# Strassen matmul with leaky ReLU on one core: the sixth product of six regions split into seven quarter products, like the seventh

## The chip, the cores and the metric

The kernel runs on one core of one Trainium2 chip. The metric is device time in microseconds (us) of one execution. The kernel before took 1568.02 us as the median of three runs (1567.33 to 1568.79).

Engines, as the profile names them: PE multiplies (its matmuls) and PEld loads the stationary operand of a matmul; DVE does elementwise sums and 32x32 transposes; ACT copies and squares; POOL and SP here only issue DMAs. PE writes its sums into PSUM, eight banks of 128 x 512 numbers in f32.

## The reference

```python
def setup_inputs():
    m, k, n = 4096, 4096, 4096
    return {"a": np.random.randn(m, k).astype(np.float32),
            "b": np.random.randn(k, n).astype(np.float32),
            "alpha": np.float32(0.01)}

def reference(a, b, alpha):
    x = np.matmul(a, b)
    return np.where(x > 0, x, alpha * x)
```

One product of two 4096 x 4096 matrices, and a leaky ReLU on the result.

## The kernel before

**Regions.** The output is cut into 16 regions of 1024 x 1024, four row groups g of four columns j. Region (0, 0) is done plainly, while the first data arrive (L279). The other 15 go through one loop (`for i, (g, j) in enumerate(regions)`, L665), the rows of a group in the order 2, 0, 1, 3 (2, 0, 3, 1 for g = 2). The last region of a group is called turning: in it the next group's rows of A are fetched and transposed. (3, 3) is the final one.

**Seven products.** In a region A is cut into 2 x 2 blocks of 512 x 2048 and B into 2 x 2 blocks of 2048 x 512, all in f16, and the four output blocks of 512 x 512 come from seven block products in place of eight (Strassen's scheme in Winograd's form). In the order of the list `PRODUCTS` their left operands are a11, a12, s2, s3, s1, a22 and s4, where s1 to s4 are sums of blocks of A; the right operands are blocks of B and sums of them, which DVE makes in place (`b_sum`, L561). A whole product is 64 matmuls of 128 x 128 by 512 columns (`product`, L672): the contraction runs over two halves k of eight chunks c each, and for each chunk over four row tiles mt, each with a PSUM bank of its own. This text counts the products from one: the sixth is a22's, the seventh s4's.

**The seventh in quarters.** In nine regions (`in_quarters`, L767: g > 0, neither turning nor final) the seventh product is cut by the same scheme once more (`quarters_product`, L696): seven quarter products of 16 matmuls with 256 columns (`part`, L707, its matmuls at L711). They need four sums of quarters of s4, made by DVE once a group (`sums_s4`, L649), kept in DRAM (`kept_s`) and loaded again by SP in the group's other two regions (L824), and four sums of quarters of B22 (`sums_b`, L640). The seven quarters follow each other in this order: two with s4 alone, then sums 4, 2, 1 and 3 of s4, and last `part(x[1, 1], f(4), onto(1, 0))` (L728). Two banks of z (`acc` is z's third, `other` its fourth) take some of the quarters; ACT copies `acc` into SBUF (L718, L721, L726) and DVE adds `other` to that (L723, L727); the rest goes straight onto y.

**Banks.** The eight PSUM banks are two sets of four, y and z. The first, third, fifth and seventh product go into y, the second into z, the fourth and sixth into z anew. The sets change places from one region to the next (`ybank`, L669): the first product of a region writes the four banks that were z in the region before. A product's results leave a bank by an ACT copy into an SBUF tile (`keep`, L690) or by a DVE add onto such a tile (`add`, L733); `leave` (L737) then does the leaky ReLU on DVE (L307) and the store on SP.

**What sets the order.** The kernel is recorded with a manual schedule: every engine and every DMA queue works through its instructions in the order of the code, and the framework adds the waits: for an operand, for a buffer or a bank still being read, and for a DMA's landing. A tile of a pool takes the buffer of its tag that comes free first. SBUF pools that matter here: x (three large buffers: s1, s4 and, by turns, s2 and the rooms of the quarter sums; s2 is kept in DRAM as `kept_s2` and loaded again at each quartered region's end, L867), a16 (three buffers of 128 x 2048 in f16: quarter sums of A, squares of `Measure`, rows of A on the way in), b (two buffers for each block of B) and c (f32 results).

**The rest.** POOL fetches the next region's blocks of B (`fetch_b`, L488), each half k as soon as its buffer is free. `Measure` (squares on ACT at L227, sums on DVE at L236 to L260) takes row and column norms of the blocks; `judge` decides with them at the end whether the f16 result stands. `MEASURED` and `EARLY` say in which region and place each block is measured.

Of the kernel before, what the change touches and what calls it, by code (L numbers as in the profile page):

```python
# [46 lines left out]
def kernel(  # L47
# [440 lines left out]
    def fetch_b(i, quads):  # L488

        if i >= len(regions):  # L490
            return
        for half, nt in quads:
            for u in (2 * half, 2 * half + 1):
                fetch_unit(i, u, nt)
# [79 lines left out]
    def judge():  # L574
# [29 lines left out]
        (1, 2): (None, [A11], None, None), (1, 0): (B21, [B22, A12], None, None),  # L604
        (1, 1): (B21, [B22, A22], None, None),
        (2, 2): (None, [A11], None, None), (2, 0): (A12, [], None, None),
        (2, 3): (B21, [B22, A22], None, None),
        (3, 2): (None, [A11], None, None), (3, 0): (A12, [A22], None, None),
    }
# [8 lines left out]
    kept_s = dram_pool.tile([4, P, KC * HALF], DT, name="kept_s")  # L618
    kept_s2 = dram_pool.tile([P, 2 * KC * RM], DT, name="kept_s2")
    side = 0  # L620

    def quarter_a(t):
        return t.rearrange("p (c m e) -> p c m e", m=HALF, e=2)

    def rooms(i):

        two = x_pool.tile([P, 2, 2, KC * HALF], DT, name="q", tag="x")
        two = [two[:, 0], two[:, 1]]
        three = [a16_pool.tile([P, KC * HALF], DT, name="sq4", tag="a16") for _ in range(3)]
        tq = {2: two[0][:, 0], 1: two[0][:, 1], 4: two[1][:, 0]}  # L630
        sq = {1: three[0], 2: three[1], 3: three[2], 4: two[1][:, 1]}
        return tq, sq

    def quarters_b(i):
        return {(k, n): have_b[i, 2 + k, 1][:, :, n * HALF:(n + 1) * HALF] for k in range(2) for n in range(2)}

    def quarters_s4(g):
        return {(h, k): s[g, "s4", k][:, :, h * HALF:(h + 1) * HALF, :] for h in range(2) for k in range(2)}

    def sums_b(i, tq):  # L640
        y = quarters_b(i)
        f = lambda n: tq[n].rearrange("p (c n) -> p c n", n=HALF)
        tt = nc.vector.tensor_tensor
        tt(y[0, 1], y[1, 1], y[0, 1], SUB)
        tt(f(2), y[0, 1], y[0, 0], ADD)
        tt(f(1), y[1, 1], f(2), SUB)
        tt(f(4), y[1, 0], f(2), SUB)

    def sums_s4(g, sq):  # L649
        x = {key: q.rearrange("p c m e -> p c (m e)") for key, q in quarters_s4(g).items()}  # L650
        f = lambda n: sq[n].rearrange("p (c m) -> p c m", m=2 * HALF)
        tt = nc.vector.tensor_tensor
        tt(f(1), x[1, 0], x[1, 1], ADD)
        tt(f(2), f(1), x[0, 0], SUB)
        tt(f(3), x[0, 0], x[1, 0], SUB)
        tt(f(4), x[0, 1], f(2), SUB)
        for n in range(4):
            nc.sync.dma_start(kept_s[n], sq[n + 1])
# [5 lines left out]

    for i, (g, j) in enumerate(regions):  # L665
        final = i == len(regions) - 1
# [5 lines left out]
        def product(n, banks, first):  # L672
            name, half, nt = PRODUCTS[n]
            todo = [(k, c) for k in range(2) for c in range(KC)]
# [3 lines left out]
            for mt, k, c in order:  # L678
                t = operand(g, name, k)
                nc.tensor.matmul(  # L680
                    banks[mt], a_cols(t, c, mt, t is first_a), B(half, nt, k)[:, c, :],
                    start=first and (k, c) == (0, 0), stop=(k, c) == (1, KC - 1), skip_group_check=not first,
                )
# [6 lines left out]
        def keep(banks, side):  # L690
            _, kept = new_c(side)
            for mt in range(MT):
                nc.scalar.copy(kept[mt], banks[mt])  # L693
            return kept

        def quarters_product(i, y, acc, other, tq, sq):  # L696

            pairs, kept = new_c(side)
            block = lambda r, n: pairs[r][:, :, n * HALF:(n + 1) * HALF]
            b = quarters_b(i)  # L700
            x = quarters_s4(g)
            f = lambda n: tq[n].rearrange("p (c n) -> p c n", n=HALF)
            into = lambda bank: [bank[:, m * HALF:(m + 1) * HALF] for m in range(2)]
            onto = lambda r, n: [y[2 * r + m][:, n * HALF:(n + 1) * HALF] for m in range(2)]
            pair = lambda bank: bank.rearrange("p (m n) -> p m n", m=2)

            def part(xq, yq, to, first=False):  # L707
                for c in range(KC):
                    for m in range(2):
                        rows = slice(m * P, (m + 1) * P)  # L710
                        nc.tensor.matmul(  # L711
                            to[m], xq[:, c // 2, rows, c % 2], yq[:, c, :],
                            start=first and (c, m) == (0, 0), stop=c == KC - 1, skip_group_check=True,
                        )

            part(x[0, 1], b[1, 0], onto(0, 0))
            part(x[0, 0], b[0, 0], into(acc), True)
            nc.scalar.copy(block(0, 0), pair(acc))  # L718
            part(quarter_a(sq[4]), b[1, 1], onto(0, 1))
            part(quarter_a(sq[2]), f(2), into(acc))  # L720
            nc.scalar.copy(block(0, 1), pair(acc))  # L721
            part(quarter_a(sq[1]), f(1), into(other), True)
            nc.vector.tensor_add(block(0, 1), pair(other), block(0, 1))  # L723
            part(quarter_a(sq[3]), b[0, 1], into(acc))
            for n in (1, 0):
                nc.scalar.copy(block(1, n), pair(acc))  # L726
            nc.vector.tensor_add(block(1, 1), pair(other), block(1, 1))  # L727
            part(x[1, 1], f(4), onto(1, 0))  # L728
# [4 lines left out]
        def add(acc, banks):  # L733
            for mt in range(MT):
                nc.vector.tensor_add(acc[mt], banks[mt], acc[mt])  # L735
# [31 lines left out]
        in_quarters = g > 0 and not turning and not final  # L767
        early = measure(i, *EARLY[g, j]) if (g, j) in EARLY else None
        if early:
            early.begin()  # L770
        if first_of_group and g:
            nc.sync.dma_start(kept_s2, whole_s[g, "s2"].rearrange("p k c m e -> p (k c m e)"))
# [6 lines left out]
        u1 = keep(y, side)  # L779
        for k in range(2):  # L780
            b_sum(B(0, 1, k), B(1, 1, k), B(0, 1, k), SUB)
            b_sum(B(0, 0, k), B(0, 1, k), B(0, 0, k), ADD)
        if middle:
            middle.end()
        fetch_a(0, 0)
# [3 lines left out]
        if first_of_group:  # L789
            sum_a(g, "s3")  # L790
        leave(u1, 0, 0)
        for k in range(2):
# [7 lines left out]
        u2 = keep(y, 1 - side)  # L800
        for k in range(2):
# [5 lines left out]
        if late_ones:  # L807
            late_ones[0].end()

        z = [new_bank(zbank + mt) for mt in range(MT)]  # L810
        product(3, z, True)
        v = keep(z, side)
        fetch_b(i + 1, [(0, 1)])
# [4 lines left out]
        if in_quarters:  # L818
            tq, sq = rooms(i)
            if first_of_group:  # L820
                sums_s4(g, sq)
            else:
                for n in (4, 2, 1, 3):
                    nc.sync.dma_start(sq[n], kept_s[n - 1])  # L824
            if len(late_ones) < 2:
                sums_b(i, tq)
# [8 lines left out]
        add(v, y)  # L835
        leave(v, 1, 1)
        if in_quarters and len(late_ones) == 2:
            sums_b(i, tq)
# [6 lines left out]
        fetch_b(i + 1, [(0, 0)])  # L845
# [3 lines left out]
        product(5, z, False)  # L849
# [103 lines left out]
```

## Time and profile before

| | |
|---|---|
| median of three runs | 1568.02 us |
| the profiled execution | 1567.84 us |
| its span, first to last instruction | 1565.9 us |
| granted clock of PE | 0.999 |
| PE, DVE, ACT, POOL busy | 1554.8, 1055.6, 372.4, 299.7 us |
| region (1, 0) from its first to the next region's first matmul | 508.03 to 603.14 us |

The profile comes from one execution, 0.18 us under the median. Its page gives each engine's busy time; the groups give, by line and shape, the number of instructions, the mean time of one and the engine's idle time ahead of them; the timeline lists instructions in order of time, neighbours of one kind merged, with start and length in us and, in brackets, idle time and what ended it. Matmuls overlap each other in the pipeline, so the 379 ns that the groups give for one is longer than the distance from one to the next; the distance is read from the timeline, as starts of consecutive groups over the number of matmuls between.

### The profile page before, as it was taken

How to read it: one execution, taken by the hardware profiler on the slowest of the kernel's cores; microseconds unless marked ns; L12 is line 12 of the kernel's file. 1: busy time of each engine (PE TensorE's matmuls, PEld its weight loads, DVE VectorE, ACT ScalarE, POOL GpSimd, SP SyncE). 2: the span in 40 equal slices, each digit the busy share in tenths (PEclk: the TensorE clock that was granted, in tenths of full speed). 3: DMA queues.
4: the chain of work that ended last, by engine and by line, in shares of the span. 5: the costliest groups of instructions: out<-in, count | busy, mean ns of one | idle time of the engine just before them, and what ended most of it. 6: DMA issues, size and time to landing. Idle time of an engine off the chain costs nothing. (4 is left out here: it accounts for less than half of the span.)

```text
span 1565.9 us, 19332 instructions
## 1 busy us (share of the span) xinstructions
PE 1554.8 (99%) x7707; PEld 753.0 (48%) x7707; DVE 1055.6 (67%) x1172; ACT 372.4 (24%) x390; POOL 299.7 (19%) x482
## 2 busy tenths in 40 slices
PE   9999999999999999999999999999999999999998
PEld 4444444444445445454444545545444454544543
DVE  4378758767975776766789682774868959372533
ACT  2201243612120334401221220531022143110110
POOL 5641110244002011023401102012330110201100
PEclk9999999999999999999999999999999999999999
DMA  9999795999829589499975949769995793949902
GB/s 244 186 217 185 151 279 150 190 194 203 284 54 246 157 167 237 92 249 209 183 275 114 276 135 174 176 140 276 168 235 203 170 260 96 217 144 193 210 27 84
DMA packets 199142, 291.84 MB, mean 186 GB/s; under 512 B 17281, under 2 KB 154753, under 8 KB 193666
## 3 DMA queue, kind: packets, MB, share of 16 engines
q0 software_dynamic: 149376, 141.59, 57.4%
q1 hardware_dynamic: 49378, 148.53, 25.4%
q8 instruction: 62, 1.02, 0.3%
q10 hardware_dynamic: 288, 0.39, 0.1%
q14 instruction: 38, 0.31, 0.1%
HBM read 341.84 MB, written 88.08 MB: 275 GB/s over the span
## 5 line engine op out<-in xcount | busy, mean ns | idle before, releaser
L680 PE MATMUL ps<-b,a 128*128 128x512 f16 x3840 | 836.1, 379 | 0.0
L680 PEld LDWEIGHTS <-a 128*128 128x128 f16 x3840 | 375.7, 98 | 451.1
L680 PE MATMUL ps<-b,s 128*128 128x512 f16 x2304 | 503.2, 379 | 0.0
L680 PEld LDWEIGHTS <-s 128*128 128x128 f16 x2304 | 225.4, 98 | 271.9
L561 DVE TENSOR_TENSOR b<-b 128x4096 f16<-128x4096 f16 x112 | 252.8, 2290 | 94.9 <-DMA b<-in_b_dram 80.0
L505 POOL DMA_DIRECT2D b<-in_b_dram x184 | 136.3, 746 | 940.9 <-PE ps L680 635.7
L735 DVE TENSOR_TENSOR c<-ps,c 128x512 f32<-128x512 f32 x180 | 111.6, 683 | 168.4 <-PE ps L680 110.1
L693 ACT COPY c<-ps 128x512 f32<-128x512 f32 x180 | 92.3, 598 | 538.5 <-PE ps L680 431.0
L139 DVE STREAM_TRANSPOSE a<-a 128x512 uint32<-128x512 uint32 (+2 forms) x120 | 126.3, 1101 | 90.5 <-DMA a<-in_a_dram 89.8
L130 POOL DMA_DIRECT2D a<-in_a_dram x252 | 137.5, 553 | 196.5 <-DVE a L139 122.5
L307 DVE SCALAR_TENSOR_TENSOR c<-c 128x512 f32<-128x512 f32 x240 | 149.5, 686 | 12.7 <-ACT c L880 10.0
L227 ACT ACTIVATE sq<-b 128x2048 bf16<-128x2048 f16 x64 | 119.1, 1910 | 89.8 <-DVE sq L236 75.8
L279 PE MATMUL ps<-b,a 128*128 128x512 f16 x512 | 112.8, 379 | 2.1 <-DMA b<-in_b_dram 0.9
L227 ACT ACTIVATE sq<-a 128x2048 bf16<-128x2048 f16 x48 | 88.8, 1921 | 77.2 <-DVE sq L236 60.3
L279 PEld LDWEIGHTS <-a 128*128 128x128 f16 x512 | 49.7, 98 | 63.0 <-issue 2.9
L718 ACT COPY c<-ps 128x512 f32<-128x512 f32 x9 | 5.3, 586 | 244.2 <-PE ps L711 244.2
L236 DVE TENSOR_TENSOR sq<-sq 128x2048 bf16<-128x2048 bf16 x27 | 33.0, 1223 | 28.8 <-ACT sq L227 28.8
L711 PEld LDWEIGHTS <-s 128*128 128x128 f16 x432 | 42.2, 98 | 6.8
L239 DVE TENSOR_TENSOR sq<-sq 128x2048 bf16<-128x2048 bf16 x27 | 33.1, 1225 | 17.2 <-ACT sq L227 17.2
L711 PEld LDWEIGHTS <-sq 128*128 128x128 f16 x432 | 42.3, 98 | 4.8
L238 DVE TENSOR_TENSOR sq<-sq 128x2048 bf16<-128x2048 bf16 x27 | 33.1, 1226 | 4.7 <-ACT sq L227 2.3
L880 ACT COPY c<-ps 128x512 f32<-128x512 f32 x24 | 12.6, 598 | 98.0 <-PE ps L680 98.0
(86 smaller groups left out, 559.7 us busy)
## 6 DMA issues: line engine op xcount, KB each, us to landing
b<-in_b_dram POOLq DMA_DIRECT2D x192, 512.0 KB, 10.5
out_dram<-c SPq DMA_DIRECT2D x240, 256.0 KB, 6.5
a<-in_a_dram POOLq DMA_DIRECT2D x244, 128.0 KB, 5.5
b<-kept SPq DMA_DIRECT2D x24, 1024.0 KB, 8.5
s<-kept_s SPq DMA_DIRECT2D x9, 2048.0 KB, 10.4
sq<-kept_s SPq DMA_DIRECT2D x18, 512.0 KB, 7.1
b<-in_b_dram POOLq DMA_DIRECT2D x24, 256.0 KB, 9.2
kept<-b SPq DMA_DIRECT2D x6, 1024.0 KB, 7.7
```

The source lines that it names most:

```text
L130: nc.gpsimd.dma_start(a16[32 * q:32 * q + 32], src.rearrange("(g i) w -> i g w", i=32))
L139: nc.vector.transpose(part.rearrange("p c m e -> p c (m e)").bitcast(U32) .rearrange("p c (g i) -> p g c i", i=32), src[:, :, i * n:(i + 1 ...
L227: nc.scalar.activation(to, self.parts[n], SQUARE)
L238: nc.vector.tensor_add(total, total, more[1])
L279: nc.tensor.matmul(ps, a_cols(at[0, h, u], c, mt, (h, u) == (0, 0)), bt[0, u, nt][:, c, :], start=first, stop=last,)
L307: nc.vector.scalar_tensor_tensor(t, t, alpha, t, op0=MULT, op1=MAX if alpha <= 1 else MIN)
L505: nc.gpsimd.dma_start(t[:, c:c + 4, :], b_rows(j, u, c, 4, nt, g > 0))
L561: nc.vector.tensor_tensor(f(to), f(x0), f(x1), op)
L680: nc.tensor.matmul(banks[mt], a_cols(t, c, mt, t is first_a), B(half, nt, k)[:, c, :], start=first and (k, c) == (0, 0), stop=(k, c) == (1 ...
L693: nc.scalar.copy(kept[mt], banks[mt])
L711: nc.tensor.matmul(to[m], xq[:, c // 2, rows, c % 2], yq[:, c, :], start=first and (c, m) == (0, 0), stop=c == KC - 1, skip_group_check=True,)
L735: nc.vector.tensor_add(acc[mt], banks[mt], acc[mt])
```

## The change

**The sixth product in quarters.** In the six quartered regions that are not the first of their group (`both`: (1, 0), (1, 1), (2, 0), (2, 3), (3, 0), (3, 1)) the sixth product becomes seven quarter products too (`sixth_in_quarters`). Sums of quarters of a22 are made once a group, in its first region, kept in DRAM (`kept_q`) and loaded in the other two. The four z banks are taken anew for it, so the fourth product, kept as v, is added to u2 in SBUF ahead of it, and the results of the seven quarters are added from PSUM onto u2 by eight adds of 128 x 512 (`more`). The sums for the seventh product follow into the same seven rooms quarter by quarter: each sum of s4 is loaded, and each sum of B22 made, when the quarter that used the room is done.

**The seventh.** Its order is now: two with s4 alone, sum 4, `x[1, 1]` with t(4), sums 2, 1 and last sum 3. Its accumulating banks are z's fourth (`one`, where `acc` was z's third) and z's second (`other`).

**k turned round.** Behind a quartered region the halves k go in the order (1, 0): fetches of B, sums of B, matmuls. s2 is loaded in two halves, the second behind the first sum of B in the next region (a small DVE memset of the room stands ahead of it).

**Moved.** s3 is made ahead of the second product. The measurements of a few blocks move to other regions.

```diff
     MEASURED = {
         (0, 1): (None, [A11], B12, B11), (0, 2): (B21, [B22, A22], B12, A12),
-        (1, 2): (None, [A11], None, None), (1, 0): (B21, [B22, A12], None, None),
-        (1, 1): (B21, [B22, A22], None, None),
-        (2, 2): (None, [A11], None, None), (2, 0): (A12, [], None, None),
-        (2, 3): (B21, [B22, A22], None, None),
+        (1, 0): (A12, [B22], None, None), (1, 1): (A22, [A11], None, None),
+        (2, 0): (B21, [A12], None, None), (2, 3): (A22, [A11], None, None),
         (3, 2): (None, [A11], None, None), (3, 0): (A12, [A22], None, None),
+        (3, 1): (B21, [B22], None, None), (3, 3): (B21, [B22], None, None),
     }
...
+    def sums_of_a(g, name, room):
...
+        def make(n, x0, x1, op):
+            made[n] = room(n)
...
+            nc.vector.tensor_tensor(f(n), f(x0), f(x1), op)
+            nc.sync.dma_start(kept_q[name][n - 1], made[n])
+
+        make(1, (1, 0), (1, 1), ADD)
+        make(2, 1, (0, 0), SUB)
+        make(3, (0, 0), (1, 0), SUB)
+        make(4, (0, 1), 2, SUB)
...
+    def load_s2(g, k, later=False):
+
+        t = s[g, "s2", k]
+        if later:
+            nc.vector.memset(t[:, 0, :1, :1], 0.0)
+        nc.sync.dma_start(t.rearrange("p c m e -> p (c m e)"), kept_s2[k])
...
+        ks = (1, 0) if in_quarters else (0, 1)
+        late_s2 = in_quarters
...
+        def sixth_in_quarters(pairs, banks, v, y, tq, sq):
...
+            one, other, third, fourth = banks
...
+            quarter_product(x[0, 0], b[0, 0], into(one), True)
+            add(v[:2], y[:2])
+            more(0, 0, one)
+            add(v[2:], y[2:])
+            quarter_product(sx(1), t(1), into(other), True)
+            more(1, 1, other)
+            following(4)
+            next_t[2] = tq[1]
+            quarter_product(x[0, 1], b[1, 0], into(fourth), True)
+            leave(v, 1, 1)
+            quarter_product(sx(2), t(2), into(one))
+            following(2)
+            more(0, 1, one)
+            sums_of_b(y7, next_t, (2,))
+            more(0, 0, fourth)
+            quarter_product(sx(4), b[1, 1], into(other))
+            following(1, sq[4])
+            next_t[4] = tq[2]
+            sums_of_b(y7, next_t, (4,))
+            more(0, 1, other)
+            quarter_product(x[1, 1], t(4), into(third), True)
+            next_t[1] = tq[4]
+            sums_of_b(y7, next_t, (1,))
+            more(1, 0, third)
+            quarter_product(sx(3), b[0, 1], into(one))
+            following(3)
+            more(1, 0, one)
+            more(1, 1, one)
+            return next_t, next_s
...
-            part(x[0, 1], b[1, 0], onto(0, 0))
-            part(x[0, 0], b[0, 0], into(acc), True)
-            nc.scalar.copy(block(0, 0), pair(acc))
-            part(quarter_a(sq[4]), b[1, 1], onto(0, 1))
-            part(quarter_a(sq[2]), f(2), into(acc))
-            nc.scalar.copy(block(0, 1), pair(acc))
-            part(quarter_a(sq[1]), f(1), into(other), True)
+            quarter_product(x[0, 1], b[1, 0], onto(0, 0))
+            quarter_product(x[0, 0], b[0, 0], into(one), True)
+            nc.scalar.copy(block(0, 0), pair(one))
+            quarter_product(sx(4), b[1, 1], onto(0, 1))
+            quarter_product(x[1, 1], t(4), onto(1, 0))
+            quarter_product(sx(2), t(2), into(one))
+            nc.scalar.copy(block(0, 1), pair(one))
+            quarter_product(sx(1), t(1), into(other), True)
             nc.vector.tensor_add(block(0, 1), pair(other), block(0, 1))
-            part(quarter_a(sq[3]), b[0, 1], into(acc))
+            quarter_product(sx(3), b[0, 1], into(one))
             for n in (1, 0):
-                nc.scalar.copy(block(1, n), pair(acc))
+                nc.scalar.copy(block(1, n), pair(one))
             nc.vector.tensor_add(block(1, 1), pair(other), block(1, 1))
-            part(x[1, 1], f(4), onto(1, 0))
             for mt in range(MT):
                 nc.vector.tensor_add(kept[mt], y[mt], kept[mt])
...
+        both = in_quarters and not first_of_group
...
+        if first_of_group:
+            sum_a(g, "s3")
         fetch_a(0, 0)
 
         product(1, z, True)
         add(u1, z)
-        if first_of_group:
-            sum_a(g, "s3")
...
+        if first_of_group and g:
+            sums_of_a(g, "a22", new_a16)
+        if in_quarters:
+            t = x_pool.tile([P, 4, QUARTER], DT, name="q", tag="x")
+            tq, sq = {2: t[:, 0], 1: t[:, 1], 4: t[:, 2]}, {4: t[:, 3]}
+        if both:
+            for n in (1, 2, 3):
+                sq[n] = new_a16()
+            load_sums("a22", sq, (1, 2, 3, 4))
...
+        if both:
+            t3_of_b(quarters_of_b(i, 1, 0))
+            sums_of_b(quarters_of_b(i, 1, 0), tq)
+            t3_of_b(quarters_of_b(i, 1, 1))
+            for mt in range(MT):
+                nc.vector.tensor_add(u2[mt], u2[mt], v[mt])
+        elif in_quarters:
+            sums_of_a(g, "s4", lambda n: sq.setdefault(n, sq[4] if n == 4 else new_a16()))
+            t3_of_b(quarters_of_b(i, 1, 1))
+            sums_of_b(quarters_of_b(i, 1, 1), tq)
...
-        product(5, z, False)
-        fetch_b(i + 1, [(1, 0)])
-        add(u2, z)
+        if not both:
+            product(5, z, False)
+            add(u2, z)
+        fetch_b(i + 1, [(1, 0)], (1, 0) if both else ks)
...
-            kept_c = quarters_product(i, y, new_bank(zbank + 2), new_bank(zbank + 3), tq, sq)
-            fetch_b(i + 1, [(1, 1)])
-            t = new_s(g, "s2")
-            nc.sync.dma_start(t.rearrange("p k c m e -> p (k c m e)"), kept_s2)
+            kept_c = seventh_in_quarters(y, new_bank(zbank + 3), new_bank(zbank + 1), tq, sq)
+            fetch_b(i + 1, [(1, 1)], (1, 0))
+            new_s(g, "s2")
+            load_s2(g, 1)
             leave(kept_c, 0, 1)
```

`quarter_product` is the old `part`; `following` takes a free a16 room (or the one named) and loads the next sum of s4 into it; `load_sums` loads sums from `kept_q`; `t3_of_b` is the in-place sum of `sums_b`, `sums_of_b` its other three; `late_s2` makes the next region's `load_s2(g, ks[1], True)` follow its first `b_sum`.

## The prediction

> **What bounds the kernel now.** First the page's busy times and the group of the whole products:
>
> ```profile
> PE 1554.8 (99%) x7707; PEld 753.0 (48%) x7707; DVE 1055.6 (67%) x1172; ACT 372.4 (24%) x390; POOL 299.7 (19%) x482
> PEclk9999999999999999999999999999999999999999
> L680 PE MATMUL ps<-b,a 128*128 128x512 f16 x3840 | 836.1, 379 | 0.0
> ```
>
> PE has no idle time ahead of these matmuls: the kernel is its stream of matmuls, and the rest costs only where it holds that stream. So I read the timeline of one quartered region, (1, 0), next: its sixth and seventh product and the next region's first.
>
> ```profile
> 577.10 13.98 PE L680 MATMUL ps<-b,a 128*128 128x512 f16 x64
> ...
> 590.91 3.66 PE L711 MATMUL ps<-b,s 128*128 128x256 f16 x32
> ...
> 599.65 1.91 PE L711 MATMUL ps<-b,sq 128*128 128x256 f16 x16
> ...
> 601.39 1.91 PE L711 MATMUL ps<-q,s 128*128 128x256 f16 x16
> 601.59 1.07 ACT L726 COPY c<-ps 128x512 f32<-128x512 f32 x2 [2.91 <-PE ps L711]
> ...
> 602.21 0.69 DVE L727 TENSOR_TENSOR c<-ps,c 128x512 f32<-128x512 f32 x1 [1.62 <-ACT c L726]
> ...
> 603.14 7.07 PE L680 MATMUL ps<-b,a 128*128 128x512 f16 x32
> ```
>
> A whole product takes 590.91 - 577.10 = 13.81 us (215.8 ns a matmul), one in quarters 603.14 - 590.91 = 12.23 (109.2 ns), a quarter 1.747. The reader should also see what happens at the end: sum 3's quarter ends at 601.39, two ACT copies and a DVE add read its banks until 602.90, and only the last quarter (601.39 to 603.14), which goes onto y, stands between that and the next region's first product, which writes these banks. The cover is 0.24 us longer than the work.
>
> The third view is the timeline of (3, 2), the first region of group 3, where DVE is fullest, then the DMA view of that stretch:
>
> ```profile
> 1236.20 1.22 DVE L653 TENSOR_TENSOR sq<-s 128x2048 f16<-128x2048 f16 x1
> 1237.45 2.71 SPq L658 DMA_DIRECT2D kept_s<-sq  x3
> ...
> 1245.66 2.48 DVE L735 TENSOR_TENSOR c<-ps,c 128x512 f32<-128x512 f32 x4
> ...
> 1259.38 2.48 DVE L735 TENSOR_TENSOR c<-ps,c 128x512 f32<-128x512 f32 x4 [8.84 <-PE ps L680]
> ...
> 1259.83 3.66 PE L711 MATMUL ps<-b,s 128*128 128x256 f16 x32
> ```
>
> ```profile
> kept_s<-sq SPq DMA_DIRECT2D x3, 512.0 KB, 5.4
> ...
> kept_s<-q SPq DMA_DIRECT2D x1, 512.0 KB, 10.9
> ```
>
> **The change part by part.**
>
> 1. *The sixth product.* Six times 13.81 becomes 12.23: 6 x 1.58 = 9.5 us less on PE. The seventh's number of matmuls stays.
>
> The Trainium skill ("TensorE: Matmul & The Clock Gate", section "Back-to-back issue gap") speaks against this: it gives about 131 ns a matmul for 512 columns and 81 for 128 as the sustained rate. Estimated from that page, 64 matmuls would take 8.4 us and 112 of 256 columns (some 98 ns) 10.9, a loss of 15 us over six regions. This trace's 215.8 and 109.2 ns decide otherwise.
>
> 2. *The hand-over at a region's end.* The seventh's order is turned: sum 3's quarter is now last. What ran under the old last quarter has no cover: when sum 3's quarter ends, ACT copies `one` (0.20 us later, 1.07 for two), DVE adds `other` behind the first copy, and ends 602.90 - 601.39 = 1.51 us after the quarter. `other` is z's second bank, and the next region's first product writes z's banks in order of mt: its first matmul goes, its second waits for that add. A matmul held by a DVE read of its bank starts 0.06 us after it (at 102.35 in the timeline, behind L318 that ended at 102.29). Without the wait it would start 0.22 after the first: 1.51 + 0.06 - 0.22 = 1.35 us of standing PE. This is in the shared code of the seventh, so in all nine quartered regions, each with a successor: 12.15 us. No other wait is there to hide it.
>
> 3. *First regions of a group.* `one` is now z's fourth bank, which the seventh's second quarter clears. `add(u2, z)` reads z in order of mt: in (3, 2) it ends at 1259.38 + 2.48 = 1261.86, while that quarter would start at 1259.83 + 1.75 = 1261.58. 0.28 + 0.06 = 0.34 us in (1, 2) and (2, 2): 0.7. In (3, 2) it is more:
>
> 4. *The sums of a22* (four DVE sums of 1.22 and four stores of 512 KB a group) stand ahead of s4's sums and share three a16 buffers with them. So a22's fourth sum waits for the landing of the first store, and s4's first, second and third for the second, third and fourth. In (1, 2) and (2, 2) A11's measurement (7.5 us of DVE) goes, and `add(u2, z)` stays on time. (3, 2) keeps it. There the first three stores take the place of the three of before and land as they did, 4.3, 5.4 and 6.4 us after issue (1241.75, 1244.15, 1246.28; the DMA view of each issue alone). a22's fourth sum ends at 1243.0; its store, with the four's mean of 6.8 us, lands at 1249.8; s4's third and fourth sum end at 1252.2, four sums of B22 (4.9) at 1257.1, `add(v, y)`, `leave` and `add(u2, z)` (2.5 each) at 1264.6. The second quarter then waits 1264.65 - 1261.58 = 3.1 us. Bounds: if that store lands 2.1 after the third (1248.4), 1.7; with 10.9 us, 7.2. I take 3.1.
>
> 5. *DVE in the six regions.* Added: four sums of B21 (4.9), four adds u2 + v (no row has f32 sums from SBUF alone; bounds 2.3, a 128 x 4096 f16 sum, and 2.8, four L727 adds; taken 2.5), eight adds of 0.69 for four (3.0 more), the memset (0.07). Cover: in (1, 0) DVE waited 8.3 us ahead of the second measurement, and that measurement (7.7) is gone. In the sixth, counted from its start, the first add from `one` ends at 2.6 and its bank is rewritten at 5.2; `other` 4.6 against 7.0; `one` again 7.9 against 10.5. If DVE came over 2.6 us late, PE would wait by the excess. Cost 0.
>
> 6. *Loads.* a22's sums are issued behind the first measurement (some 52 us into the region) and used from 70.8: cover 18, median of such a load 7.1. Of s4's, sum 3 has least: its room is free when the sixth ends, and it is read 10.5 us later. The loads of such sums before landed within 3.2 to 8.1. Cost 0, margin about 2. v's stores, now behind sum 4's load on SP, and u2's, behind sum 3's, are late by under 3 us; the copy that needs v's room comes at 15.9 from the sixth's start, they land near 14.
>
> 7. *k turned round.* B22's second half is fetched by POOL 1.7 us later (what follows on POOL is the next region's fetches, 40 us off); its sums ended 26.0 us into a region at worst, and with the turned order that half is needed at 34.5. s2's second half waits on SP for the memset at about 17 and needs 8.5 (a 1 MB load) by 34.5; behind it stand stores that are not ready. Cost 0. In a turning region the added 1.35 us on PE favours the transposes of A.
>
> 8. *Moved.* s3 ahead of the second product's add: in (2, 2) that add ends 4.5 us later, at 38.0, needed at 41.4. Measurements in (3, 3) fall where DVE waited 24.7 us for PE; `judge` is behind, unchanged. Cost 0.
>
> Sum: 1567.84 - 9.5 + 12.15 + 0.7 + 3.1 = 1574.3 for the profiled execution, which lay 0.18 under the median: 1574.5.
>
> **The rivals.**
>
> *The hand-over is not held* (the other side). If PE's second matmul were let through, because the add had no part in its wait or the bank came free earlier, parts 1, 3 and 4 remain: 1562.3. It decides from 0.63 us a region: (9.5 - 3.8) / 9; over that the change loses. For it: before, nothing was held there. Against: then a quarter of 1.75 us lay between, and the same copies and add took 1.51 each of nine times.
>
> *Loads or DVE late in the six regions.* Sum 3 lands late, or DVE is behind at the sixth. A landing of 12 us, as B's fetches have (10.5 median, up to 21 in the busiest stretch), holds PE 1.7 us in each: 1574.5 + 10 = 1584.7. For it: the DMA engines are over 90% busy in most of that stretch. Against: SP's loads landed within 8.1 beside the same fetches.
>
> *(3, 2) costs almost nothing*, its stores landing faster: 1571.8, or under 1571 if the hand-over is also a little cheaper.
>
> *The clock falls.* The kernel's first matmuls (1.19 to 4.58 us) stand 427 ns apart, twice the later distance. Should the 3 us wait in (3, 2) bring that back for the 3.4 us it lasted then, half of that time is lost: 1576.2. Against: waits of up to 1.3 us early on did not. The Trainium skill ("TensorE: Matmul & The Clock Gate", Part 1) has the clock halved after an idle window of about 3.4 us; no row before has so long a wait.
>
> That the change does not do what it says I leave out: PE's order has 288 more matmuls, six times 48.
>
> **How the numbers follow.** Forecast, 1571.5 to 1579: 0.58. Clock: 0.06, inside it. Loads or DVE late: 0.14. (3, 2) free and the hand-over cheaper, within 0.2% (0.2%, 3.1 us, is what a measurement of this kernel can tell): 0.12. Not held: 0.10. So faster 0.10, same 0.12, slower 0.78. The range for 8 in 10 runs from 1568, half into the case of no change, to 1583, which leaves out half of the late loads.
>
> **What would show it.** Right: a gap of about 1.35 us between the first and second matmul of the first product behind each of nine regions, ended by the DVE add that is `other`'s last; sixth products of 12.2 us without gaps; one wait of about 3 us near the seventh's start in (3, 2), with DVE waiting for stores of `kept_q`. Wrong: no such gaps (1562), or PE waiting for DMAs of sums inside the sixth and seventh.

## The result

The kernel after took 1578.82 us (median of five executions, 1577.32 to 1582.41), beside 1567.50 for the kernel before (five, 1567.26 to 1568.79): a ratio of 1.0073 [1.0058, 1.0088], slower by 11.3 us. The prediction had 1574.5 us, 1568 to 1583. Two executions of the comparisons further down, one of the kernel before (3858 us) and one of the second experiment (5364 us), took more than twice as long as all others and are left out of the medians and ratios.

The profiled execution took 1580.19 us, with a span of 1578.3 and a granted clock of 0.998. From the kernel after's page: the engines' busy time, the group of the whole products, and the group of B's transfers (512 KB each, median us from issue to landing).

```profile
PE 1549.3 (98%) x7995; PEld 781.1 (49%) x7995; DVE 1127.2 (71%) x1265; ACT 373.3 (24%) x390; POOL 299.6 (19%) x482
...
L722 PE MATMUL ps<-b,a 128*128 128x512 f16 x3456 | 754.3, 379 | 11.3 <-DVE c L808 10.7
...
b<-in_b_dram POOLq DMA_DIRECT2D x192, 512.0 KB, 13.5
```

PE is busy 5.5 us less than before, with the 288 matmuls more that were predicted; but ahead of the whole products, where before it had no idle time, it now has 11.3 us, and 10.7 of them are ended by the DVE add at L808, `other`'s last. The third line answers to 10.5 us before. It was not among the lines that the prediction watched, and turned out to matter.

The timeline of the end of (1, 0), which the prediction showed for the kernel before, is now:

```profile
602.69 1.91 PE L673 MATMUL ps<-b,q 128*128 128x256 f16 x16
...
604.43 0.38 PE L722 MATMUL ps<-b,a 128*128 128x512 f16 x1
604.63 1.07 ACT L807 COPY c<-ps 128x512 f32<-128x512 f32 x2 [2.91 <-DMA out_dram<-c]
...
605.25 0.69 DVE L808 TENSOR_TENSOR c<-ps,c 128x512 f32<-128x512 f32 x1 [1.62 <-ACT c L807]
...
606.00 1.25 PE L722 MATMUL ps<-b,a 128*128 128x512 f16 x5 [1.19 <-DVE c L808]
```

Sum 3's quarter ends at 604.43, one matmul of the next region goes, and the next one starts at 606.00, 1.57 us later instead of 0.22: 1.35 us. The same gap stands behind all nine quartered regions.

**Where the time is.** In a stream of matmuls any wait shows as a distance longer than the unheld one (215.8 ns for 512 columns, 109.2 for 256). The table takes the loop from its first to its last matmul, less all of these unheld distances: what is left is what PE lost. The unheld time is 1435.7 us before and 1426.3 after, so that the quarters save 9.48 us as such.

| what PE lost in the loop, us | before | after |
|---|---|---|
| second matmul behind a quartered region, 9 x 1.35 | 0 | 12.15 |
| seventh's second quarter in (1, 2) and (2, 2) | 0 | 0.69 |
| the same quarter in (3, 2) | 0 | 3.94 |
| slower matmuls behind that wait | 0 | 1.66 |
| fourth product in (1, 3) | 0 | 1.05 |
| all, with small differences | 0.17 | 19.74 |

So the loop is 1435.90 us before and 1445.99 after, 10.1 more. The spans differ by 12.4: the loop starts 1.2 us later in this execution, and its end, from the last matmul to the last store's landing, is 1.1 longer. Other kernels with this same start and end, below, began at 122.2 to 123.9 us, where before has 122.8 and after 124.0, and ended 7.2 to 8.1 us after the start of their last matmul, where before has 7.2 and after 8.3, so these 2.3 us look like chance of one execution. The medians differ by 11.3, 1.2 more than the loop; this remainder stays open.

The lines that answer to (3, 2), timeline of the kernel after:

```profile
1246.65 1.23 DVE L657 TENSOR_TENSOR q<-a,q 128x2048 f16<-128x2048 f16 x1 [1.85 <-DMA kept_qa<-q]
...
1252.99 1.23 DVE L657 TENSOR_TENSOR q<-q,s 128x2048 f16<-128x2048 f16 x1 [3.01 <-DMA kept_qa<-q]
1255.87 1.23 DVE L657 TENSOR_TENSOR q<-s 128x2048 f16<-128x2048 f16 x1 [1.65 <-DMA kept_qa<-q]
...
1264.58 1.91 PE L673 MATMUL ps<-b,s 128*128 128x256 f16 x16
...
1267.73 2.48 DVE L815 TENSOR_TENSOR c<-ps,c 128x512 f32<-128x512 f32 x4
...
1270.27 3.41 PE L673 MATMUL ps<-b,s 128*128 128x256 f16 x16 [3.78 <-DVE c L815]
```

DVE makes the sums of a22 and s4 and waits for the landing of the stores of `kept_q`, as predicted; `add(u2, z)` (the L815 line) comes late, and PE waits for it. What follows stands in the windows of this stretch (columns: busy us and instructions of each engine, then PE's granted clock, DMA share, GB/s):

```profile
1266.30:1270.20 3.90, 0.19 (x2) 0.02 (x1) 3.90 (x8) 0.00 (x0) 0.22 (x1) 1.00 1.22 219
1270.20:1273.60 3.40, 3.33 (x17) 2.44 (x17) 2.42 (x5) 0.00 (x0) 0.00 (x0) 0.54 1.14 286
1273.60:1282.00 8.40, 8.40 (x78) 7.43 (x77) 0.69 (x1) 1.17 (x2) 1.49 (x2) 0.98 1.16 274
```

Right behind the wait the clock is granted at 0.54 for 3.4 us, and 16 matmuls stand 213 ns apart instead of 109.

And the fourth product of the turning region (1, 3), same kernel's timeline:

```profile
718.63 2.29 DVE L561 TENSOR_TENSOR b<-b 128x4096 f16<-128x4096 f16 x1 [13.01 <-DMA b<-in_b_dram]
...
739.31 2.10 DVE L139 STREAM_TRANSPOSE a<-a 128x512 uint32<-128x512 uint32 x2 [2.94 <-DMA a<-in_a_dram]
...
741.33 2.44 DVE L815 TENSOR_TENSOR c<-ps,c 128x512 f32<-128x512 f32 x4
...
743.23 0.38 PE L722 MATMUL ps<-b,a 128*128 128x512 f16 x1 [0.22 <-DVE c L815]
...
743.83 2.53 PE L722 MATMUL ps<-b,a 128*128 128x512 f16 x11 [0.22 <-DVE c L815]
```

DVE's first `b_sum` starts 19.3 us into the region, after 13 us of waiting for B. In the kernel before, where the region starts at 698.25, it is 14.3:

```profile
712.57 4.69 DVE L561 TENSOR_TENSOR b<-b 128x4096 f16<-128x4096 f16 x2 [9.76 <-DMA b<-in_b_dram]
```

In the kernel after, four transposed pieces of the next A follow the sums of B, so `add(u1, z)` begins only at 741.33, and the fourth product, due at 742.12, is held three times for the banks of z.

### The profile page after: what moved, and what is told of

It reads as the page before. It is cut to its first block, busy times and chain, and to the rows that moved or that the text cites. A ratio compares the mean times of both kernels' runs of the same rounds, so it can differ in the third digit from the quotient of the medians.

```text
span 1578.3 us, 20106 instructions
## 1 busy us (share of the span) xinstructions
PE 1549.3 (98%) x7995; PEld 781.1 (49%) x7995; DVE 1127.2 (71%) x1265; ACT 373.3 (24%) x390; POOL 299.6 (19%) x482
## 3 DMA queue, kind: packets, MB, share of 16 engines
q1 hardware_dynamic: 56290, 167.41, 28.6%
q8 instruction: 64, 1.05, 0.3%
## 5 line engine op out<-in xcount | busy, mean ns | idle before, releaser
L722 PE MATMUL ps<-b,a 128*128 128x512 f16 x3456 | 754.3, 379 | 11.3 <-DVE c L808 10.7
L722 PEld LDWEIGHTS <-a 128*128 128x128 f16 x3456 | 337.3, 98 | 420.0 <-DVE c L808 14.2
L735 ACT COPY c<-ps 128x512 f32<-128x512 f32 x180 | 92.3, 598 | 484.3 <-PE ps L722 422.7
L815 DVE TENSOR_TENSOR c<-ps,c 128x512 f32<-128x512 f32 x156 | 97.0, 681 | 85.7 <-PE ps L722 59.2
L279 PE MATMUL ps<-b,a 128*128 128x512 f16 x512 | 113.0, 379 | 2.8 <-DMA b<-in_b_dram 1.4
L673 PEld LDWEIGHTS <-q 128*128 128x128 f16 x960 | 94.1, 98 | 11.1
L279 PEld LDWEIGHTS <-a 128*128 128x128 f16 x512 | 49.7, 98 | 63.9 <-issue 3.4
L798 ACT COPY c<-ps 128x512 f32<-128x512 f32 x9 | 5.3, 586 | 263.8 <-PE ps L673 263.8
L673 PE MATMUL ps<-b,q 128*128 128x256 f16 x480 | 57.5, 273 | 0.0
L804 DVE TENSOR_TENSOR c<-ps,c 128x512 f32<-128x512 f32 x9 | 6.2, 691 | 58.1 <-issue 49.8
L239 DVE TENSOR_TENSOR sq<-sq 128x2048 bf16<-128x2048 bf16 x27 | 33.1, 1225 | 17.4 <-ACT sq L227 17.4
L673 PE MATMUL ps<-q,q 128*128 128x256 f16 x384 | 45.4, 273 | 0.0
## 6 DMA issues: line engine op xcount, KB each, us to landing
b<-in_b_dram POOLq DMA_DIRECT2D x192, 512.0 KB, 13.5
```

What stands on the lines that cost most here:

```text
L239: nc.vector.tensor_add(total, total, self.held[3])
L279: nc.tensor.matmul(ps, a_cols(at[0, h, u], c, mt, (h, u) == (0, 0)), bt[0, u, nt][:, c, :], start=first, stop=last,)
L673: nc.tensor.matmul(to[m], xq[:, c // 2, rows, c % 2], yq[:, c, :], start=first and (c, m) == (0, 0), stop=c == KC - 1, skip_group_check=True,)
L722: nc.tensor.matmul(banks[mt], a_cols(t, c, mt, t is first_a), B(half, nt, k)[:, c, :], start=first and (k, c) == todo[0], stop=(k, c) == t ...
L815: nc.vector.tensor_add(to, bank, to)
```

## The experiments

The theory from these traces: four separate places hold PE, and each can be taken away by itself. The main rival to it: the waits are signs of one thing, DVE or the transfers running late in general, so that a wait removed in one place comes back in the next.

### The hand-over: free banks first

```diff
             order = [(mt, k, c) for k, c in todo for mt in range(MT)]
+            if n == 0 and late_s2:
+                order = [(mt, k, c) for free in ((0, 2), (1, 3)) for k, c in todo[:4] for mt in free]
+                order += [(mt, k, c) for k, c in todo[4:] for mt in range(MT)]
```

> The changed kernel with one thing added: behind a quartered region, the first product runs its first four chunks on z's first and third bank (free by then) before it goes to the second and fourth, so that 8 matmuls, 1.73 us, lie over the two ACT copies and the DVE add that end 1.51 us after the seventh. Theory (hand-over of 1.35 us in nine regions is most of the loss): all nine gaps vanish, -12.15 us; the waits that DVE sets in the turning region (1, 3) grow by up to 1.35, because PE is earlier there: 1567 to 1569 where the changed kernel has 1578.8. Rival A (the gaps only show a loss that loads of B set anyway; PE would wait later in the region): 1575 or more, with new gaps ended by DMAs or DVE. Rival B (no loss at the hand-over): no change, 1578.8.

It took 1566.61 us (eleven executions, 1563.89 to 1569.4), a ratio of 0.9989 [0.998, 0.9998] to before. In the timeline of this kernel the add at 602.59 (L811 here) comes as late behind the quarter as in the kernel after, and no matmul waits for it:

```profile
601.77 4.48 PE L725 MATMUL ps<-b,a 128*128 128x512 f16 x20
601.97 1.07 ACT L810 COPY c<-ps 128x512 f32<-128x512 f32 x2 [2.91 <-DMA out_dram<-c]
...
602.59 0.69 DVE L811 TENSOR_TENSOR c<-ps,c 128x512 f32<-128x512 f32 x1 [1.62 <-ACT c L810]
```

All nine gaps of 1.35 us are gone, and the median fell by 12.2, a little more than the theory had. The lag itself is not what costs; that the second matmul asks for a bank that is not free yet, while two others are, is. The main rival is not without ground here: in the profiled execution, the longest of the eleven, the loop is only 9.3 us shorter (1436.70), because (3, 2) loses 7.2 us where it lost 5.6, the fourth product in (2, 1) now waits 0.76 us, and two loads of sums in (1, 1) come 0.35 late. In (1, 3), where a growth of up to 1.35 us was expected, the waits are 1.09.

### The hand-over: sum 3's quarter not last

```diff
             quarter_product(sx(4), b[1, 1], onto(0, 1))
-            quarter_product(x[1, 1], t(4), onto(1, 0))
...
             nc.vector.tensor_add(block(1, 1), pair(other), block(1, 1))
+            quarter_product(x[1, 1], t(4), onto(1, 0))
```

> The changed kernel with the seventh's order as it was: the quarter that goes onto y with t(4) is last again, sums 2, 1 and 3 each come a quarter earlier. Theory: the nine hand-over gaps vanish (-12.15 us), but sum 3 is now read 8.7 us after the sixth's end in place of 10.5, and in the changed kernel's profile it landed 8.3 to 10.2 us after: PE waits about 3 us in all for it and for sum 1, over the six regions, at quarters that now read them. 1578.8 - 12.15 + 3 = 1569.7, and up to 1.35 more in (1, 3). Rival A (loss set by loads of B): 1575 or more. If the loads do not hold PE: 1566.7.

It took 1570.44 us (median of eleven executions, 1565.56 to 1574.6), a ratio of 1.0015 [1.0004, 1.0025]. The nine gaps are gone here too, but the median fell by 8.4 us only, for the quarters with sums 2, 1 and 3 now read them 1.75 us earlier, and the loads have that much less time. In 14 places of the six regions the seventh now loses 0.06 to 0.93 us, 4.5 together where about 3 were expected, on them. The largest, in (1, 1):

```profile
689.08 1.16 PE L673 MATMUL ps<-q,q 128*128 128x256 f16 x9 [0.76 <-DMA q<-kept_qs]
```

So what the changed kernel's order of the last quarters gives away at the end it saves in the middle: the two orders trade 12.15 us of hand-over for 4.5 us of late loads. The prediction's rival of late loads is right in this much: the loads had almost no spare time left.

### The hand-over in the kernel before

```diff
             nc.vector.tensor_add(block(0, 1), pair(other), block(0, 1))
+            part(x[1, 1], f(4), onto(1, 0))
             part(quarter_a(sq[3]), b[0, 1], into(acc))
             for n in (1, 0):
                 nc.scalar.copy(block(1, n), pair(acc))
             nc.vector.tensor_add(block(1, 1), pair(other), block(1, 1))
-            part(x[1, 1], f(4), onto(1, 0))
```

> The kernel before with nothing but the order of the seventh's last two quarters exchanged, so that sum 3's is last. Its banks are z's third (two ACT copies, free 1.27 us after) and fourth (DVE add, 1.51 us after). Theory by banks: the next first product runs two matmuls and waits at its third for ACT, 1.27 + 0.06 - 0.43 = 0.90 us, then hardly at its fourth: 0.92 us in nine regions, +8.3 us on 1567.5: 1575.8. With z's second bank, as in the changed kernel, it would be 12.15; that the sum is less shows that the order of the banks sets it. Rival (the first product waits for the whole of the copies and adds): +12 or more. Rival (no hold): 1567.5.

It took 1576.12 us (1575.24 to 1576.67), a ratio of 1.0051 [1.0037, 1.0064]. The exchange of two quarters alone, without any of the rest of the change, costs 8.2 us. Timeline at the end of (1, 0):

```profile
604.56 0.59 PE L680 MATMUL ps<-b,a 128*128 128x512 f16 x2
604.76 1.07 ACT L727 COPY c<-ps 128x512 f32<-128x512 f32 x2 [4.66 <-PE ps L711]
...
605.89 4.28 PE L680 MATMUL ps<-b,a 128*128 128x512 f16 x19 [0.73 <-ACT c L727]
```

In this kernel `acc` is z's third bank. Two matmuls go and the third waits, for ACT, 0.89 us nine times: 8.0. The price of the hand-over is thus the bank order and the lag, 0.89 us where the third bank is the first that is still read, 1.35 where it is the second.

### The measurement in (3, 2)

```diff
-        (3, 2): (None, [A11], None, None), (3, 0): (A12, [A22], None, None),
-        (3, 1): (B21, [B22], None, None), (3, 3): (B21, [B22], None, None),
+        (3, 2): (None, [], None, None), (3, 0): (A12, [A22], None, None),
+        (3, 1): (B21, [B22], None, None), (3, 3): (B21, [B22, A11], None, None),
```

> The changed kernel with A11's measurement moved from (3, 2) to the final region (all that is computed stays). Theory: DVE is 7.5 us earlier in (3, 2), add(u2, z) is on time, the wait at the seventh's second quarter falls from 3.94 us to the 0.35 that (1, 2) and (2, 2) have, and the clock does not fall after it (17 matmuls at half the rate, 1.7 us): -5.3 us, 1573.5. Rival (the slow matmuls have nothing to do with the wait): -3.6, 1575.2, with the slow stretch still there. Rival (stores of the sums set it, not the measurement): no change.

It took 1572.09 us (eleven executions, 1570.63 to 1572.6), a ratio of 1.0025 [1.0016, 1.0034]: 6.7 less than the kernel after. In this kernel's timeline the wait in (3, 2) is down to the 0.34 us of the other two groups:

```profile
1262.55 2.48 DVE L815 TENSOR_TENSOR c<-ps,c 128x512 f32<-128x512 f32 x4 [3.47 <-PE ps L722]
...
1263.00 1.91 PE L673 MATMUL ps<-b,s 128*128 128x256 f16 x16
...
1265.09 1.91 PE L673 MATMUL ps<-b,s 128*128 128x256 f16 x16 [0.18 <-DVE c L815]
```

No matmul of 256 columns stands 213 ns from the next there, and the mean granted clock of the execution is 0.999. That separates the two parts of the loss: with the wait the slow matmuls go as well. It also gives the size of the second: the loop lost 19.74 us in the kernel after and 13.85 here, and of these 5.9 the wait is 3.6 and the slow matmuls 1.66 (the rest is a shorter wait in the turning regions, 0.45 for 1.05). Where the wait stayed, each profiled execution shows slow matmuls behind it, but not equally many: 16 in the kernel after (wait 3.94 us), 26 in the first experiment (4.36), 12 in the second (4.27). The Trainium skill ("TensorE: Matmul & The Clock Gate", Part 1) has the clock halved after an idle window of about 3.4 us, and that window runs freely. That agrees with 3.94 us setting it off and 1.35 not, and with the differing lengths, whose cause no run here settles.

### The sixth product whole again

```diff
-        both = in_quarters and not first_of_group
+        both = False
```

> The kernel after, with the sixth product taken whole again in the six regions; the seventh's order, the k turned round, the half loads of s2, the sums of A22 in the first regions of a group and the moved measurements stay. The theory (quarters in the sixth save 1.58 us of TensorE in each of six regions, all of it on the path): six sixth products of 13.81 us where the kernel after has 12.23, so +9.5; the seventh's second quarter then waits for the last addition of the sixth in six more regions, 0.34 us each as the trace of the kernel after shows it in (1,2) and (2,2), so +2.0; the added loads and stores of the sixth are gone, so that the 1.05 us of waits in the turning region (1,3) go or shrink. From 1578.8: 1589.3 to 1590.3. The transfers of B land in 10.5 to 11.5 us (median) where the kernel after has 13.5. The rival (the quarters in the sixth cost as much on the other engines as they save, and the whole loss is elsewhere) expects 1579 to 1582.

It took 1588.66 us (four executions, 1586.85 to 1590.4), a ratio of 1.0131 [1.0115, 1.0146], 9.8 above the kernel after and just under the 1589.3 to 1590.3 expected; the loop is 10.4 us longer, 1456.41 against 1445.99, where +9.5, +2.0 and -1.05 made 10.45. All three terms show: 1435.7 us of unheld distances, a wait of 0.34 us at the seventh's second quarter in the six regions, and none in the turning regions. The quarters in the sixth earn all of their 9.5 us. The transfers of B came to 11.7 us, a little over the 10.5 to 11.5 expected.

### The loads of sums, doubled in the kernel before

```diff
-                for n in (4, 2, 1, 3):
+                for n in (4, 2, 1, 3, 4, 2, 1, 3):
                     nc.sync.dma_start(sq[n], kept_s[n - 1])
```

> The kernel before, in which each of the four loads of a seventh's sum (0.5 MB each, on the queue of SyncE, in the fourth product) is issued twice in the six regions that load them: 24 loads or 12.6 MB more, with the compute unchanged. The theory (the first transfers of B for the turning region (1,3) come late because the added loads of sums share the DMA engines with them): the median of B's transfers rises from 10.5 us to 11.5 to 13.5, and the first b_sum in (1,3) waits for B some microseconds more than before (there it begins 14.3 us into the region), to 16 to 20 us; no wait of TensorE, or up to 1 us, so 1567.9 to 1569. The rival (the B transfers are late in the kernel after because its issues were moved, not because of the bytes) expects the median at 10.5 to 11 and b_sum at 14.3 us.

It took 1570.96 us (1569.81 to 1573.46), a ratio of 1.0019 [1.001, 1.0028], 2.7 above before, where at most 1 was expected on PE. B's transfers took 11.8 us, and its profile has in (1, 3), which starts at 697.84:

```profile
718.52 4.69 DVE L561 TENSOR_TENSOR b<-b 128x4096 f16<-128x4096 f16 x2 [16.12 <-DMA b<-in_b_dram]
...
739.39 2.44 DVE L735 TENSOR_TENSOR c<-ps,c 128x512 f32<-128x512 f32 x4
...
740.09 0.38 PE L680 MATMUL ps<-b,a 128*128 128x512 f16 x1 [0.65 <-DVE c L735]
```

`b_sum` starts 20.7 us into the region, where the kernel before has 14.3. The same happens in (2, 1), and PE loses 3.5 us in the two. The transfer that this `b_sum` waits for, in the traces of four kernels (the last column is the experiment above, the sixth product whole again):

| | before | loads doubled | after | after, sixth whole |
|---|---|---|---|---|
| issued, us ahead of the start of (1, 3) | 5.56 | 5.56 | 5.79 | 5.79 |
| from issue to landing, us | 19.8 | 26.1 | 25.0 | 14.4 |
| first `b_sum`, us into the region | 14.3 | 20.7 | 19.3 | 8.8 |
| bytes on SP's queue, MB | 148.53 | 161.12 | 167.41 | 154.83 |

The rival falls: the transfer is issued no later in the kernel after. With the same issue, 12.6 MB more on SP's queue (304.43 MB in all for 291.84) make it land 6.3 us later, and with it the fourth product comes late. The last column shows the same from the other side: the kernel with the sixth product whole keeps the seventh's new order, the halves of k turned round and the half loads of s2, but not the 12.6 MB of the sixth's loads, and there the transfer, issued as early as in the kernel after, lands 10.6 us sooner. The Trainium skill ("Trainium Kernel Development and Optimization", Key Constraints) has the DMAs of SP, ACT and POOL run on the same 16 DMA engines; this run agrees.

### The last piece of A later

```diff
-        fetch_a(0, 0)
+        fetch_a(0, 0, slice(3))
 
         product(1, z, True)
         add(u1, z)
+        fetch_a(0, 0, slice(3, None))
```

> The kernel after with one edit: in the turning regions (1,3) and (2,1) the last piece of the next A's first quarter is fetched and transposed behind add(u1, z) instead of ahead of it. The theory (in the kernel after DVE reaches add(u1, z) in (1,3) so late, behind a first b_sum that waits for B and four transposed pieces, that the fourth product waits for the banks): add(u1, z) comes 2.1 us earlier, the three waits of 1.05 us together are gone, the first b_sum still waits for B (11 to 13 us), and the stretch from the loop's first matmul to the last one goes from 1446.4 us to 1445.3; time 1577.8, or 1576.6 if the 1.2 us by which the kernel after's median stood above what its loop explains was an accident of those executions. The rival (the fourth product's waits come from the mean speed of the A transfers, and return for the piece that is moved) expects the loop at 1446.4 and waits of TensorE elsewhere in (1,3).

It took 1577.98 us (1576.82 to 1579.3), a ratio of 1.0065 [1.0051, 1.0079]. DVE's timeline in (1, 3) has the add ahead of the fourth piece:

```profile
718.15 2.29 DVE L561 TENSOR_TENSOR b<-b 128x4096 f16<-128x4096 f16 x1 [12.68 <-DMA b<-in_b_dram]
...
735.55 2.44 DVE L815 TENSOR_TENSOR c<-ps,c 128x512 f32<-128x512 f32 x4
738.02 2.10 DVE L139 STREAM_TRANSPOSE a<-a 128x512 uint32<-128x512 uint32 x2
```

B is about as late as in the kernel after (19.0 us into the region), but the add comes 5.8 us earlier, in place of the 2.1 expected: by the piece itself, 2.1, by that piece's own wait of 2.94 for A, and by the rest of B's earlier landing and of smaller waits. PE has no wait left in a turning region. The expected length of the loop was missed all the same. The expectation counted to the last matmul's end, 0.38 us after its start: so counted, the loop is 1446.45 us, where the kernel after has 1446.37 and 1445.3 was expected. That is the rival's figure, 1446.4, but by accident: the rival wanted new waits in (1, 3), and there are none. In this execution the wait in (3, 2) was 4.36 us, not 3.94, and 21 matmuls behind it stood at 213 ns, not 16, which took back 1.1. Its median cannot decide whether the open 1.2 us of the kernel after is real; it is 0.84 lower, where 1.05 (real) and 2.2 (chance) were the choices, and with (3, 2) differing by as much, neither is excluded.

### Four edits together

The kernel after with the free banks first, the measurement moved, the last piece of A later, and in the first region of a group the two accumulating banks of the seventh exchanged:

```diff
-            kept_c = seventh_in_quarters(y, new_bank(zbank + 3), new_bank(zbank + 1), tq, sq)
+            one, other = (1, 3) if first_of_group else (3, 1)
+            kept_c = seventh_in_quarters(y, new_bank(zbank + one), new_bank(zbank + other), tq, sq)
```

> The kernel after with four edits together: behind a quartered region the first product's first four chunks go to the banks 0 and 2 and then 1 and 3; the measurement of A11 goes from (3,2) to (3,3); in the turning regions the last piece of the next A's first quarter is fetched and transposed behind add(u1, z) instead of ahead of it; and in the first region of a group the seventh takes z's second bank for its first blocks and the fourth for the single one. The theory, from the kernel after's 1578.8 and its trace: the nine waits of 1.35 us go (-12.15), in (3,2) the 3.94 us wait and the 1.7 us of slower matmuls go (-5.6), the three waits of 0.35 us at the seventh's second quarter go (-1.0), the waits of 1.05 us for add(u1, z) in (1,3) go (-1.05): 1559.0, and 1557 to 1560 with what the start and the last stores differ from run to run. The rival (where a wait is taken away, the next one ends as late: the sums' loads or DVE) expects 1563 to 1568.

It took 1558.85 us (five executions, 1557.87 to 1559.46), beside 1568.23 for the kernel before: 0.9939 [0.9925, 0.9952]. It beats both kernels. Its page:

```profile
PE 1546.1 (99%) x7995; PEld 781.3 (50%) x7995; DVE 1127.4 (72%) x1265; ACT 373.7 (24%) x390; POOL 300.4 (19%) x482
...
L725 PE MATMUL ps<-b,a 128*128 128x512 f16 x3456 | 752.3, 379 | 0.0
...
b<-in_b_dram POOLq DMA_DIRECT2D x192, 512.0 KB, 13.7
```

No idle time ahead of the whole products; the loop, 1426.38 us, loses 0.13 us beyond its unheld distances, as little as before. So the 9.5 us of the sixth product are all there in the time (1568.23 - 1558.85 = 9.4), and no wait came back elsewhere, though B's transfers are as slow as in the kernel after: with the add ahead of the last piece their lateness is covered. The rival expected 1563 to 1568. The exchanged banks were not run by themselves; with the four edits the waits at the seventh's second quarter are gone.

## Why the prediction was right, and where its sum was not

The direction and three of the terms stood; the sum was 4.3 us short of the measured time, which lies 0.2 us under the upper end of the forecast's range.

- **Part 1, the sixth product, -9.5:** right. The unheld distances of the loop fall by 9.48, and whole products in its place cost them again.
- **Part 2, the hand-over, 9 x 1.35:** right to the hundredth, in cause (L808) and place (the second matmul). The seventh's turned order and the order of the next product's banks are both needed for it: either one, changed alone, takes the gaps away.
- **Part 3, 0.34 us in (1, 2) and (2, 2):** right; 0.35 and 0.34.
- **Part 4, (3, 2), 3.1 us (1.7 to 7.2):** the mechanism was right, the size 3.94. From the first sum of a22 to the end of s4's last, the working had 16.0 us (1236.2 to 1252.2); the trace has 17.0 (1241.18 to 1258.2): the stores that the eight sums wait for landed later by so much.
- **The clock:** a rival at 0.06, inside the forecast's range, that came true. It was priced at 1.7 us for a 3 us wait, and cost 1.66 in the profiled execution; that the two agree is partly luck, as the four other executions below that have such a wait lost 1.3 to 2.8. Its argument against, that waits of up to 1.3 us did not lower the clock, was no evidence on a wait three times as long; the rival should have had a larger chance, as part 4's own bounds reached to 7.2 us.
- **Part 6, loads, "Cost 0, margin about 2":** the cost of PE's own waits on loads was 0, but the margin was not 2. Sum 3 of s4 landed 8.3 to 10.2 us after the seventh's start and is read at 10.48, so 0.26 us was left in (1, 1); the second experiment, which reads it 1.75 us earlier, waits there.
- **Part 7, "In a turning region the added 1.35 us on PE favours the transposes of A":** this is the step that failed. The loads were asked only whether they land in time themselves, not what they do to transfers that share the DMA engines with them. The bytes on SP's queue went from 148.53 to 167.41 MB, the transfers of B from 10.5 to 13.5 us, and the turning region, where `b_sum`, four transposed pieces and `add(u1, z)` stand in one line on DVE, passed that on to PE: 1.05 us in (1, 3). The doubled loads show it in the kernel before, and the kernel with the sixth product whole shows it the other way.
- **Parts 5 and 8, cost 0:** nothing on PE speaks against them; no gap lies inside the sixth product, and none in (2, 2)'s second.

The three misses (0.84 in part 4, 1.66 of clock, 1.05 in (1, 3)) make 3.55 of the 3.6 us by which the loop's loss, 10.1, exceeds the predicted 6.45. The rest of the 4.3 is the open 1.2 us of the medians, less the 0.5 by which the kernel before came out lower in this comparison than in the runs that the prediction was given.

## What to carry to other kernels

When the last step of a stage is exchanged, look at which bank or buffer the next stage asks for first: an order that starts on the free ones hid 1.35 us nine times, at no cost. Loads added to a queue that has room were not free for the transfers of another queue here; price them by what their bytes do to the slowest transfer, and by what stands in line behind that transfer. In this kernel a wait of PE near 4 us is to be counted with a third to two thirds of its length again for the clock.

## What was not expected of the hardware

The cost of a long wait goes on after its end, and varies. In the five profiled executions that have it, a wait of 3.85 to 4.36 us in (3, 2) was followed by 12 to 26 matmuls at 213 ns instead of 109, while the 1.35 us waits never were. The kernels that keep the wait also spread more: eleven executions of the first experiment lie within 5.5 us and eleven of the second within 9.0, against 2.0 for eleven of the fourth, where the wait is 0.34 (eleven with the doubled loads, without such a wait, lie within 3.7). The granted clock of each execution speaks for the clock as the cause: in each of the five kernels that have the wait, the longest execution has the lowest clock of its kernel (0.996 or 0.997), and all eleven of the fourth have 0.999. No run varied the clock by itself, so this is not shown.

Loads by SP delayed POOL's transfers of B more than each other. With 12.6 MB more in the kernel before, B's median rose from 10.5 to 11.8 us, and the transfer ahead of (1, 3) took 6.3 us more, while the median of the sums' loads stayed at 7.1.
